# Attention in a hybrid backbone kernel: the transposes of two key tiles issued in one place instead of two

## The chip, the cores and the metric

The kernel runs on one core of one Trainium2 chip. The metric is the device time of one execution in microseconds; the time before the change is the median of three runs. PE is TensorE (PEld its weight loads), DVE is VectorE, ACT is ScalarE, POOL is GpSimd and SP is SyncE, whose queue issues most DMAs.

## The reference, cut to what matters

Two layers over 2048 latent tokens and 256 context tokens. The first is a gated MLP with spatial mixing, the second is windowed attention. Only the attention is touched by the change. For each block of 128 queries, each of 16 heads (4 heads share one set of keys and values) sees the keys of its own block, the block on each side, all 256 context keys and a sink logit:

```python
s_loc = jnp.where(valid, jnp.einsum('bqhgd,bkhd->bhgqk', qb, kb) * scale, NEG_INF)
s_ctx = jnp.einsum('bqhgd,bkhd->bhgqk', qb, k_ctx) * scale
p = jax.nn.softmax(jnp.concatenate([s_loc, s_ctx, s_sink], axis=-1), axis=-1)
out = p_loc @ vb + p_ctx @ v_ctx          # then out * silu(z), the output projection and a layer norm
```

Arithmetic is fp32. The kernel splits an operand into a rounded high part and a low rest, and multiplies the parts on PE.

## The kernel before, in words

Attention is the last stage, from about 2139 us to the end. It goes over 16 query blocks. A block has four **units**, one for each set of keys, and a unit covers four heads. A unit's keys are 5 tiles of 128 (4 in the first and last block), and one key tile of one unit is a **step**: 16 steps in block 0, 20 in each of blocks 1 to 14, 16 in block 15, so 312 in all. Below, the steps of a block of 20 are called 0 to 19; its units begin at steps 0, 5, 10 and 15, and every block begins at an even step of the whole count.

What belongs to a unit and a step:

- `s_mm` (L1087, four matmuls, L1096 to L1099): the scores of one head, into `pS`. `s_max` (L1102, DVE, L1107): adds the mask and finds the extreme. `s_exp` (L1111, ACT, L1115): the exponentials and their sum, in place in the tile `S`; a second, short instruction reads out the sum. Four heads of the next unit are prepared during the steps of the present one.
- `t_mm` (L1118): the four 128x128 transposes (L1122) of a step, one for each head, into one tile `pT` of a PSUM pool that has two buffers (L1030).
- `t_hi` (L1124, ACT, helper line L121): reads `pT` and writes the high part `ph`. `t_lo` (L1129, DVE, helper line L124): `pl` = `pT` minus `ph`. `pl` is the last reader of `pT`, so that a `t_mm` waits for the `pl` of two steps earlier, the last user of its buffer.
- `pv_mm` (L1134, L1139 and L1140): two matmuls of `ph` and `pl` with the values into `pO`, two steps later. After a unit's last tile `o_copy` (L1142, ACT, L1145, tile `ot`) and `o_add` (L1147, DVE, L1151, two additions into `oT`) clear `pO`.
- `out_piece` (L1201, L1216 to L1218): three matmuls of the output projection of the block before into `pY`. The layer norm of that block runs on DVE, ACT (`x`, L575) and POOL (L578, L579). `z_den` (L1157) makes the softmax's denominators on DVE (`es`, L1166) and ACT.

The order on each engine is written out by hand. Every piece of work is entered into a list with a due time in steps, the list is sorted by due time (equal times in the order of entry), and PE, ACT, DVE and POOL each run their instructions in just that order: an instruction that waits holds up all that is behind it on its engine. Within a step s the due times are: `t_mm` at s + 0.25, a score group at s + 0.45, `t_hi` at s + 0.5, the `exp` at s + 0.55, `t_lo` at s + 0.8, `s_max` at s + 0.9, and `pv_mm` of step s at s + 2 (that of a unit's first tile at s + 2.9). At a unit's start at step s the products of the last unit's last tile stand at s + 1, its `o_copy` at s + 1.25 and its `o_add` at s + 1.5.

Of the kernel before, what the change touches and what calls it, by code (L numbers as in the profile page):

```python
# [49 lines left out]
def kernel(  # L50
# [97 lines left out]
    def kk_of(g):  # L148
        return 4 if GROUPS[g][1] == 256 else 2
# [9 lines left out]
    def at(th, g, k):  # L159
        return th[g, k // kk_of(g)][:, k % kk_of(g)]  # L160
# [829 lines left out]
    for g in range(1, NG):  # L990
        s = start_of[0, g - 1]
# [7 lines left out]
    for n in range(1, 5):  # L999
        s, step = start_of[n - 1, 4], 4 * W3  # L1000
        if n == 1:
            s, step = s + 32 * N3, 2 * W3
# [7 lines left out]
    for k in range(7):  # L1010
        s = start_of[4, 2] + 5.4 * k
# [38 lines left out]
    def len_keys(b):  # L1050
        return 4 if b in (0, NB - 1) else 5
# [255 lines left out]
        if ui:  # L1307
            at(first_step[ui - 1] - 3, load_unit, b, kv)
    for s, (b, kv, j) in enumerate(steps):
        at(s + 0.25, t_mm, b, kv, j)  # L1310
        at(s + 0.5, t_hi, b, kv, j)
        at(s + 0.8, t_lo, b, kv, j)
        p = s + 2
        if s >= NS - 2:
            p = NS + (-0.5, 0.6)[s - NS + 2]
        elif s == NS - 3:
            p = NS - 1
        at(p + (0.9 if j == 0 else 0), pv_mm, b, kv, j)
        if j == len_keys(b) - 1:
            fast = b == NB - 1 and kv == 3  # L1320
            at(p + (0.05 if fast else 0.25), o_copy, b, kv)
            at(p + (0.1 if fast else 0.5), o_add, b, kv)
# [37 lines left out]
    b, e = NB - 1, NS  # L1360
# [88 lines left out]
```

## Time and profile before

| | |
|---|---|
| three runs | 2779.89, 2782.4, 2782.86 us (median 2782.4) |
| the profiled execution | 2783.28 us, of it 2781.5 us from the first to the last instruction |
| granted TensorE clock, mean | 0.997 of full speed |
| busy over the span | PE 2734.1 us (98%), DVE 1615.7 (58%), ACT 956.3 (34%), POOL 593.6 (21%) |
| share of the chain of work that ended last | PE 90%, DVE 6%, DMA 2%, ACT 1% |
| from 2500 to 2600 us (inside attention), busy of 100 us | PE 98.09, DVE 87.31, ACT 76.34, POOL 39.78 |

A row of the timeline gives the start, the time it took, the engine, the line, the operation, what is written and read, the shape and the count; in brackets stands the idle time of the engine before it and what ended it. Matmuls are pipelined: four transposes in one row with "0.60" are four starts and the last one's end, and the next row can start before that end. The table shows shares of the whole program; attention's own shares are those of its last line.

### The profile page before, as it was taken

The page shows a single profiled execution, that of the slowest core. Times are in us where ns is not written, and L with a number is a line of the kernel's source. Part 1 is how long each engine was busy: PE and PEld are TensorE (multiplying, and loading weights), DVE is VectorE, ACT ScalarE, POOL GpSimd, SP SyncE. Part 2 cuts the span into 40 slices and gives each one's busy share as a digit, 9 for nine tenths or more (in the row PEclk, how much of TensorE's full clock was granted, in tenths as well). Part 3 has the DMA queues.
Part 4 walks back from the last instruction along what each step waited for, and adds up shares of the span by engine and source line. Part 5 has one row for each costly group of instructions (what it writes and reads, how often), then busy time and mean ns, then how long its engine had stood idle before and what let it go on. Part 6 is the DMA issues. An engine that isn't in the chain of part 4 may idle for free.

```text
span 2781.5 us, 37612 instructions
## 1 busy us (share of the span) xinstructions
PE 2734.1 (98%) x13896; PEld 2321.7 (83%) x13896; DVE 1615.7 (58%) x3225; ACT 956.3 (34%) x1854; POOL 593.6 (21%) x498
## 2 busy tenths in 40 slices
PE   7999999999999999999999999999998999999998
PEld 6788888888888888888888888888887888888886
DVE  7531226556566555465555555455334888888887
ACT  5320222112122112132111113322223777777775
POOL 0000002223222222221111111122100333433343
PEclk9999999999999999999999999999999999999999
DMA  8631332223223323235333336533344444434442
GB/s 318 199 96 50 99 89 92 86 89 106 81 86 106 92 80 98 68 125 180 107 117 114 117 125 225 200 122 110 110 140 137 148 125 132 132 120 125 132 122 69
DMA packets 283069, 338.54 MB, mean 122 GB/s; under 512 B 24579, under 2 KB 190851, under 8 KB 282886
## 3 DMA queue, kind: packets, MB, share of 16 engines
q1 hardware_dynamic: 244006, 316.10, 35.3%
q10 hardware_dynamic: 38880, 20.05, 2.5%
q8 instruction: 109, 1.79, 0.3%
q14 instruction: 74, 0.61, 0.1%
HBM read 232.25 MB, written 103.83 MB: 121 GB/s over the span
## 4 chain that ended last, share of the span: by engine, by line
PE 90%; DVE 6%; DMA 2%; ACT 1%; issue 1%; POOL 0%; SPq 0%; DVEq 0%; ACTq 0%; POOLq 0%
PE pu L376 5%; PE pu L377 5%; PE pv L232 5%; PE pu L378 5%; PE pv L233 5%; PE pv L234 5%; PE pt L740 5%; PE pt L741 5%; PE pt L739 5%; PE pz L376 5%; PE po L618 5%; PE pz L377 5%; PE pz L378 5%; PE po L619 5%; PE po L621 5%; PE pT L1122 4%
## 5 line engine op out<-in xcount | busy, mean ns | idle before, releaser
L124 DVE TENSOR_TENSOR pl<-pT,ph 128x512 fp32r<-128x512 f32 x312 | 214.3, 687 | 79.6 <-ACT ph L121 75.8
L376 PE MATMUL pu<-hh,wuh 128*128 128x512 f32 (+1 forms) x640 | 240.4, 376 | 0.0
L232 PE MATMUL pv<-wvh,hh 128*128 128x512 f32 x576 | 225.2, 391 | 14.6 <-ACT hh L121 14.6
L377 PE MATMUL pu<-hh,wul 128*128 128x512 f32 (+1 forms) x640 | 236.1, 369 | 0.0
L378 PE MATMUL pu<-hl,wuh 128*128 128x512 f32 (+1 forms) x640 | 235.7, 368 | 0.0
L376 PE MATMUL pz<-hh,wzh 128*128 128x512 f32 (+1 forms) x640 | 235.4, 368 | 0.0
L377 PE MATMUL pz<-hh,wzl 128*128 128x512 f32 (+1 forms) x640 | 235.4, 368 | 0.0
L378 PE MATMUL pz<-hl,wzh 128*128 128x512 f32 (+1 forms) x640 | 235.4, 368 | 0.0
L739 PE MATMUL pt<-kh,wbh 128*128 128x512 f32 (+1 forms) x592 | 228.8, 386 | 0.0
L740 PE MATMUL pt<-kh,wbl 128*128 128x512 f32 (+1 forms) x592 | 228.7, 386 | 0.0
L741 PE MATMUL pt<-kl,wbh 128*128 128x512 f32 (+1 forms) x592 | 228.6, 386 | 0.0
L618 PE MATMUL po<-woh,yh 128*128 128x512 f32 x576 | 226.6, 393 | 1.7 <-ACT yh L121 1.7
L619 PE MATMUL po<-wol,yh 128*128 128x512 f32 x576 | 225.1, 391 | 0.0
L233 PE MATMUL pv<-wvl,hh 128*128 128x512 f32 x576 | 224.9, 390 | 0.0
L234 PE MATMUL pv<-wvh,hl 128*128 128x512 f32 x576 | 224.8, 390 | 0.0
L621 PE MATMUL po<-woh,yl 128*128 128x512 f32 x576 | 221.8, 389 | 0.0
L1107 DVE CUSTOM_DVE_ANT_0 S<-pS,mask 128x640 f32<-128x640 f32 (+1 forms) x252 | 216.9, 861 | 3.7 <-PE pS L1099 3.7
L1115 ACT ACTIVATE S<-S,nm 128x640 f32<-128x640 f32 (+1 forms) x240 | 196.7, 820 | 56.4 <-DVE nm L1107 56.2
L467 POOL TENSOR_TENSOR u<-u,z 128x512 f32<-128x512 f32 (+1 forms) x80 | 107.5, 1344 | 490.8 <-DVE z L466 484.7
L121 ACT ACTIVATE ph<-pT 128x512 fp32r<-128x512 f32 x312 | 184.9, 593 | 71.7 <-PE pT L1122 68.3
L1122 PE MATMUL pT<-ident,S 128*128 128x128 f32 x1232 | 186.3, 273 | 9.8 <-DVE pl L124 8.3
L1122 PEld LDWEIGHTS pT<-ident,S 128*128 128x128 f32 x1232 | 151.6, 141 | 46.8 <-DVE pl L124 10.9
(224 smaller groups left out, 5991.2 us busy)
## 6 DMA issues: line engine op xcount, KB each, us to landing
vscr<-vt ACTq DMA_DIRECT2D x72, 256.0 KB, 2.3
yr<-yscr SPq DMA_DIRECT2D x72, 256.0 KB, 3.1
ar<-in_dram SPq DMA_DIRECT2D x64, 256.0 KB, 2.8
vr<-vscr SPq DMA_DIRECT2D x64, 256.0 KB, 2.7
yscr<-y SPq DMA_DIRECT2D x64, 256.0 KB, 2.4
q<-qscr SPq DMA_DIRECT2D x64, 256.0 KB, 3.7
wor<-in_dram SPq DMA_DIRECT2D x46, 256.0 KB, 2.9
kh<-khscr SPq DMA_DIRECT2D x56, 192.0 KB, 3.3
```

Of the source, the lines that this page charges most:

```text
L232: T.matmul(ps, hk[:, cs], wh, start=first, stop=False)
L233: T.matmul(ps, hk[:, cs], wl, start=False, stop=False)
L234: return T.matmul(ps, lk[:, cs], wh, start=False, stop=last)
L376: T.matmul(ps[:, 0:tn], w[0][:, k], at(hh, g, k), start=(k == 0), stop=False)
L377: T.matmul(ps[:, 0:tn], w[1][:, k], at(hh, g, k), start=False, stop=False)
L378: T.matmul(ps[:, 0:tn], w[0][:, k], at(hl, g, k), start=False, stop=(k == KD - 1))
L618: T.matmul(pss[hf], hi[:, c % 4], wh[:, cs], start=(c == 0), stop=False)
L619: T.matmul(pss[hf], hi[:, c % 4], wl[:, cs], start=False, stop=False)
L739: T.matmul(ps, wh[:, cs], at(kh, g, k), start=(k == 0), stop=False)
L740: T.matmul(ps, wl[:, cs], at(kh, g, k), start=False, stop=False)
L741: T.matmul(ps, wh[:, cs], at(kl, g, k), start=False, stop=(k == KD - 1))
L1122: T.transpose(pt[:, hq * P:hq * P + P], u["st"][hq][0][:, j * P:j * P + P], ident)
```

## The change

Step s issued its own transposes at s + 0.25. Now an odd step's transposes are due one step earlier, at the same time as those of the even step ahead of it, and come directly behind them on PE. So eight transposes go out together, into both buffers of `pT`, at every even step, and none at an odd step. All other due times stay.

```diff
     for s, (b, kv, j) in enumerate(steps):
-        at(s + 0.25, t_mm, b, kv, j)
+        at(s - s % 2 + 0.25, t_mm, b, kv, j)
         at(s + 0.5, t_hi, b, kv, j)
         at(s + 0.8, t_lo, b, kv, j)
```

## Rows read from the trace of the kernel before

**Rows 1.** The page's costliest groups: the transposes (busy, mean ns; idle before, releaser).
```profile
L1122 PE MATMUL pT<-ident,S 128*128 128x128 f32 x1232 | 186.3, 273 | 9.8 <-DVE pl L124 8.3
```

**Rows 2.** Windows by stage: stretch, us, busy by engine, PEclk, DMA share, GB/s.
```profile
2139.00:2150.00 11.00, 8.73 (x53) 8.03 (x54) 6.59 (x16) 6.12 (x14) 0.00 (x0) 0.85 0.66 209
...
2180.00:2300.00 120.00, 118.71 (x712) 103.63 (x711) 102.11 (x223) 93.03 (x192) 43.56 (x33) 1.00 0.40 121
...
2700.00:2745.00 45.00, 43.72 (x268) 37.78 (x267) 37.78 (x87) 33.79 (x72) 19.43 (x14) 1.00 0.30 90
```

**Rows 3.** Waits of PE, 2139 to 2782 us: us in total, times, longest.
```profile
PE pT L1122 <- DVE pl L124: 8.3, 13, 0.6
PE pO L1140 <- DVE pl L124: 4.6, 4, 2.8
...
PE pT L1122 <- ACT S L1115: 1.6, 2, 1.1
```

**Rows 4.** Waits of DVE and ACT in the same stretch.
```profile
DVE pl L124 <- ACT ph L121: 75.8, 112, 2.5
ACT ph L121 <- PE pT L1122: 68.3, 124, 3.9
```

**Rows 5.** Timeline of PE, steps 0 to 2 of one block.
```profile
2489.97 0.60 PE L1122 MATMUL pT<-ident,S 128*128 128x128 f32 x4
2490.32 0.42 PE L1096 MATMUL pS<-kh,q 128*128 128x384 f32 x1
2490.58 0.34 PE L1097 MATMUL pS<-kl,q 128*128 128x384 f32 x1
...
2491.23 0.39 PE L1140 MATMUL pO<-pl,vc 128*128 128x512 f32 x1
2491.46 0.60 PE L1122 MATMUL pT<-ident,S 128*128 128x128 f32 x4
...
2493.19 0.60 PE L1122 MATMUL pT<-ident,S 128*128 128x128 f32 x4
```

**Rows 6.** Timeline of ACT, the same steps.
```profile
2491.82 0.19 ACT L1115 ACTIVATION_READ_ACCUMULATOR S<-S,nm 128x1 f32 x1
2492.03 0.60 ACT L1145 ACTIVATE ot<-pO 64x512 f32<-64x512 f32 x1
```

**Rows 7.** Timeline of DVE, the same steps.
```profile
2492.66 0.85 DVE L1151 TENSOR_TENSOR oT<-pO,ot 64x256 f32<-64x256 f32 x2
2493.54 0.69 DVE L124 TENSOR_TENSOR pl<-pT,ph 128x512 fp32r<-128x512 f32 x1
```

**Rows 8.** Timeline of PE, the transposes of steps 4, 6 and 7 of that block.
```profile
2497.44 0.60 PE L1122 MATMUL pT<-ident,S 128*128 128x128 f32 x4
...
2501.93 0.60 PE L1122 MATMUL pT<-ident,S 128*128 128x128 f32 x4
...
2503.76 0.66 PE L1122 MATMUL pT<-ident,S 128*128 128x128 f32 x4 [0.64 <-DVE pl L124]
```

**Rows 9.** Timeline of ACT, steps 4 and 5.
```profile
2498.24 0.19 ACT L1115 ACTIVATION_READ_ACCUMULATOR S<-S,nm 128x1 f32 x1
2498.33 0.58 ACT L121 ACTIVATE ph<-pT 128x512 fp32r<-128x512 f32 x1
...
2498.91 1.24 ACT L575 ACTIVATE x<-x,bnb,brs 128x1024 f32<-128x1024 f32 x1
```

**Rows 10.** Timeline of POOL, the layer norm of an earlier block.
```profile
2500.22 2.40 POOL L578 TENSOR_TENSOR x<-x,st 128x1024 f32<-128x1024 f32 x1 [2.27 <-ACT x L575]
```

**Rows 11.** Timeline of DVE, steps 3 to 5.
```profile
2497.97 0.68 DVE L124 TENSOR_TENSOR pl<-pT,ph 128x512 fp32r<-128x512 f32 x1
...
2499.55 0.88 DVE L1107 CUSTOM_DVE_ANT_0 S<-pS,mask 128x640 f32<-128x640 f32 x1
...
2500.35 2.30 DVE L1166 TENSOR_TENSOR es<-es,l 128x8 f32<-128x8 f32 x1
...
2503.05 0.65 DVE L124 TENSOR_TENSOR pl<-pT,ph 128x512 fp32r<-128x512 f32 x1
```

## The prediction

> **What bounds the kernel now.** I read the windows by stage first. From 2180 to 2745 us, the steady part of attention, PE is busy 97 to 99% of each stretch at a granted clock of 1.00, DVE about 85%, ACT 75 to 78% [rows 2]. So PE sets the end, and what the change can win is what PE still waits. The waits of PE come next: 8.3 us of transposes waiting for DVE's `pl`, in 13 places of 0.64 us, one in nearly every block; 4.6 us of products in 4 places and 1.6 us on the exponentials in 2 [rows 3]. Against that stand idle times that cost nothing today: DVE 75.8 us until `ph`, ACT 68.3 us until the transposes [rows 4]. Last I read the timelines of PE, ACT and DVE through one block, because with two `pT` buffers the question is when each `pl` lands.
>
> **The change, part by part.**
>
> *The transposes themselves.* No instruction is added or removed, no DMA moves, and SP and POOL are passed by nothing. A group of four holds PE for 0.44 us: the next row starts 0.35 us after it (2489.97 to 2490.32) and then needs 0.42 where its like needs 0.34 [rows 5]. If the extra 0.08 were a switch from transposes to other matmuls, joining 156 pairs would save 156 x 0.08 = 12.5 us. But four transposes take 0.60 us and one takes 273 ns [rows 1, 5], so that they start (600 - 273) / 3 = 109 ns apart, and 0.44 / 4 is 110 ns: the 0.08 is the fourth transpose's own time. I take nothing, and keep 12.5 us of gain for the range.
>
> *The new wait.* The odd step's group needs the buffer of the odd step before, so it waits for that step's `pl`. Until now it had a whole step's work of PE in front of it. Now it has one group, 0.44 us. Behind it in PE's queue wait scores (and so `s_max` and the exponentials), a projection piece and products.
>
> At steps 2 and 3 I lay the same rows out in the new order. The pair at step 0 starts at 2489.97 as before. The products of the last unit's last tile ended at 2491.23 + 0.39 = 2491.62 [rows 5] and now end one group later, at 2492.06. ACT is free at 2491.82 + 0.19 = 2492.01 and started `ot` at 2492.03 [rows 6]; now it starts at about 2492.09, 0.03 us behind the products, as `oT` starts 0.03 us behind `ot` (2492.63 to 2492.66). `oT` follows 0.63 us after `ot`'s start and `pl` of step 1 0.88 us after that [rows 6, 7], so that `pl` runs from 2493.60 to 2494.29. From `pl`'s end to the transposes that waited for it is 0.06 us (2503.70 to 2503.76) [rows 8, 11], so step 3's group can start at 2494.35. PE has done the same work up to step 2, in another order, and starts that group at 2493.19 [rows 5]; it is ready for step 3's at 2493.63. **PE waits 0.72 us.** That happens where a unit begins at an even step, that is at steps 3 and 13, twice in each of 14 blocks: 28 x 0.72 = 20.2 us.
>
> *Step 5* is the first tile of a unit, and its transposes, one step earlier, need the fourth head's exponentials. These end at 2498.24 + 0.19 = 2498.43 [rows 9], and the group would have come at 2497.44 + 0.44 = 2497.88 [rows 8], a wait of 0.6 us. But PE is by then 0.72 us later and the DVE and ACT work that leads there only 0.06, so nothing is left.
>
> *Steps 6 and 7.* Here PE waits 0.64 us already, since `pl` of step 5 is late: ACT's layer norm ends at 2500.15, POOL's L578 starts at 2500.22, and DVE's tiny `es` addition, begun 0.13 us later, lasts until L578 is done, 2.30 us [rows 9 to 11]. In the new order step 4's transposes start 0.72 us later, at 2498.16, and `ph` 0.63 us after that (0.60 and the same 0.03), 0.46 us after its old start [rows 8, 9]. The layer norm, L578, `es` and `pl` of step 5 move with it, and `pl` ends at 2503.70 + 0.46 = 2504.16; step 7's group can start at 2504.22. PE reaches it at 2501.93 + 0.72 + 0.44 = 2503.09 [rows 8], since the scores that stood between steps 6 and 7 (0.67 - 0.08 = 0.59 us) now come behind. It waits 1.13 us. Group and scores end at 2504.22 + 0.44 + 0.59 = 2505.25 instead of 2504.20, so that PE is now 1.05 us late and not 0.72: 0.33 us more in 13 blocks, 4.3 us. The bounds are 0 and 0.75 (with the old times of `pl`, 1.39 less 0.64), or 0 to 9.8 us.
>
> *The other pairs.* `pl` of the odd step comes earlier than now, since its transposes do, and PE comes later; I take 0. *Blocks 0 and 15* have eight units that begin at even steps: up to 8 x 0.72 = 5.8 us, while the 4.6 + 1.6 = 6.2 us of waits that don't repeat by block [rows 3] could go. I take 0 between these.
>
> **Sum.** 20.2 + 4.3 = 24.5 us on the profiled execution's own 2783.28 us, which gives 2807.8; that execution is 0.9 us over the median of the runs shown, so the forecast is 2807 us.
>
> **The rivals.**
>
> *The `es` addition gets in front of L578.* It begins 0.13 us behind it [rows 10, 11], and both move. `s_max`, which holds `es` up, starts when `pl` of step 4 is off DVE. If DVE comes out 0.13 us or more ahead, `pl` of step 5 is some 2 us earlier and step 7's wait is gone: PE's lag there falls from 1.05 to -0.08 us, 13 x 1.13 = 14.7 us less, or 2792. For it speaks how narrow the margin is; against it, that both hang on step 4's `ph` and move together.
>
> *No catching up.* If each `pl` stays where it is, every pair pays what today's times show: at step 2, 2494.23 + 0.06 - 2493.63 = 0.66; at step 4, 2498.65 + 0.06 - 2497.88 = 0.83; at step 6 a net 0.75; at step 12 about as much as at step 2 [rows 5, 7, 8, 11]. That is 2.9 us a block, 41 us or 2823, and more with the pairs not shown. It holds where ACT and DVE are short of time, not just kept waiting; rows 4 speak against it.
>
> *The lead pays off (not slower).* The odd steps' transposes are ready early, ACT and DVE use up idle time [rows 4] and no `pl` is late any more. Then the 8.3 and 1.6 us of waits of rows 3 go: 2772. Its point is DVE's queue ahead of `pl` of step 1: that `pl` must end by 2493.57, 0.72 us sooner than laid out. Against it: `pl` follows `oT` by 0.03 us, with no idle time before it [rows 7], and `oT` depends on products that the change puts later.
>
> *The clock falls.* Today it reads 1.00 with 13 waits of 0.64 us, and 0.85 only at the stage's start, among waits of up to 2.8 us [rows 2, 3]; there it cost 0.15 x 11 = 1.65 us. One such loss a block would add 23 us, 2830. The longest wait that I lay out is 1.13 us, so I give it little. The Trainium skill (TensorE: Matmul & The Clock Gate, "A second HAM failure mode: psum-queue depth-cycling") tells of a kernel in which brief idle times between groups of matmuls that cycled through PSUM banks made the clock swing between its levels. By that rule the time would be this rival's; the trace before, which has such waits at full clock, does not agree so far.
>
> That the change does something else than it says I leave out: equal due times keep the order of entry.
>
> **How the numbers follow.** Forecast 0.64, `es` in front 0.14, no catching up 0.10, the lead pays off 0.08, clock 0.04. The forecast's own range is 2797 (step 7 costs nothing, half of the 12.5 us is real) to 2818 (9.8 us at step 7, 5.8 in the outer blocks). To hold 8 in 10 I reach to the `es` case below, 2790, and to the no-catching-up case above, 2826. A measurement can tell about 0.2%, 5.6 us, from no change. Faster has 0.05, from the lead; the same 0.07, 0.03 from the lead and 0.04 from the `es` case's lower edge; slower 0.88.
>
> **What would show it.** Right: waits of the transposes on `pl` rise from 8.3 us to 35 or more (20.2 + 13 x 1.13 = 34.9, and some in the outer blocks), as 0.72 us at steps 3 and 13 and 1.1 at step 7, the second group alone waiting; ACT's waits on transposes fall; the clock stays at 1.00; a block takes some 1.8 us more. Wrong: `es` at 0.17 us in most blocks (the first rival), waits at steps 5, 9 or 15 (no catching up), or PE's waits below 10 us.

## The result, and the profile after

The changed kernel takes 2813.83 us (median of 4 runs, 2809.97 to 2815.72) against 2782.18 us (4 runs, 2779.89 to 2782.86) for the kernel before: a ratio of 1.0114, 95% interval 1.01 to 1.0129. It is slower by about 32 us, where 2807 us had been forecast. The profiled execution took 2812.83 us, 29.55 us more than the one of before; its mean granted clock is again 0.997.

All of the loss is in attention. From one block's first transposes to the next's, the block of [rows 5] took 39.6 us and now takes 41.6. Blocks 1 to 14 together went from 554.4 to 580.7 us, 26.3 us more; the rest of the 29.55 us lies in blocks 0 and 15.

PE's waits from 2139 us to the end (us in total, times, longest), to be held against [rows 3]:

```profile
PE pT L1122 <- DVE pl L124: 44.4, 48, 3.5
PE pS L1097 <- DMA kl<-klscr: 0.9, 1, 0.9
PE pS L1096 <- DVE pl L124: 0.8, 1, 0.8
```

13 waits of 8.3 us have become 48 of 44.4 us. In blocks 1 to 14 they stand in three places only: step 3 (14 times), step 13 (14 times) and step 7 (13 times). The other seven are in blocks 0 and 15. The 4.6 us of products waiting for `pl` are gone from the table. It lists idle time of PE, so a group that starts late while the last transposes are still under way is not in it; step 5 below is such a place.

The windows by stage show the other side (us, busy by engine, clock, DMA share, GB/s), to be held against [rows 2]: every engine is less busy in a stretch, and the clock has not moved.

```profile
2180.00:2300.00 120.00, 114.52 (x679) 100.04 (x678) 96.44 (x209) 87.61 (x183) 40.67 (x30) 1.00 0.40 118
...
2700.00:2745.00 45.00, 42.59 (x254) 37.16 (x253) 36.15 (x78) 32.56 (x69) 15.56 (x11) 1.00 0.39 121
```

**Steps 0 to 3**, in the same block as [rows 5 to 7]. PE, with the eight transposes of steps 0 and 1, the second of the last unit's two products, and the transposes of steps 2 and 3:

```profile
2505.89 1.03 PE L1122 MATMUL pT<-ident,S 128*128 128x128 f32 x8
...
2507.58 0.40 PE L1140 MATMUL pO<-pl,vc 128*128 128x512 f32 x1
...
2509.10 0.60 PE L1122 MATMUL pT<-ident,S 128*128 128x128 f32 x4
2510.36 0.63 PE L1122 MATMUL pT<-ident,S 128*128 128x128 f32 x4 [0.66 <-DVE pl L124]
```

ACT, then DVE, over the same steps:

```profile
2508.02 0.60 ACT L1145 ACTIVATE ot<-pO 64x512 f32<-64x512 f32 x1
```

```profile
2508.65 0.85 DVE L1151 TENSOR_TENSOR oT<-pO,ot 64x256 f32<-64x256 f32 x2
2509.52 0.69 DVE L124 TENSOR_TENSOR pl<-pT,ph 128x512 fp32r<-128x512 f32 x1
```

Read from the first transposes, at 2505.89: the products end at 2507.98, `ot` starts 0.04 us after that, `oT` 0.63 us after `ot`, `pl` of step 1 0.87 us after `oT`, and `pl` ends at 2510.21, which is 4.32 us in. The second group of the next pair would have been ready at 2509.10 + 0.44 = 2509.54 and starts at 2510.36. The stall is 0.82 us. The row's bracket says 0.66, because it counts from the end of the last transpose (2509.70), which comes 0.16 us after PE could have begun the next.

**Steps 4 to 7**, to be held against [rows 8 to 11]. PE:

```profile
2514.17 1.24 PE L1122 MATMUL pT<-ident,S 128*128 128x128 f32 x8
...
2518.75 0.60 PE L1122 MATMUL pT<-ident,S 128*128 128x128 f32 x4
2520.40 0.63 PE L1122 MATMUL pT<-ident,S 128*128 128x128 f32 x4 [1.06 <-DVE pl L124]
```

POOL, then DVE:

```profile
2516.77 2.40 POOL L578 TENSOR_TENSOR x<-x,st 128x1024 f32<-128x1024 f32 x1 [2.83 <-ACT x L575]
```

```profile
2513.96 0.68 DVE L124 TENSOR_TENSOR pl<-pT,ph 128x512 fp32r<-128x512 f32 x1
...
2516.91 2.29 DVE L1166 TENSOR_TENSOR es<-es,l 128x8 f32<-128x8 f32 x1
...
2519.61 0.65 DVE L124 TENSOR_TENSOR pl<-pT,ph 128x512 fp32r<-128x512 f32 x1
```

The pair of steps 4 and 5 takes 1.24 us where that of steps 0 and 1 takes 1.03: step 5's group starts 0.15 us behind `pl` of step 3, which ends at 2514.64, and so 0.18 us late. It is 0.18 to 0.21 us late in blocks 2 to 14, 2.5 us in all, and the table of waits has none of it.

L578 still gets in ahead of `es`, by 0.14 us where it was 0.13, and `es` ends when L578 does, 0.03 us after it, in each of these 13 blocks. The Trainium skill (GPSIMD Engine Reference, "8. Key points") says that GpSimd shares its SBUF interfaces with VectorE, with contention for VectorE instructions that have two SBUF inputs; `es` is one, and the rows agree (2.29 us beside L578, 0.17 us where no POOL instruction runs). The price that the rows show is the whole remainder of the POOL instruction: in block 15, where `es` starts 1.45 us behind L578, it takes 0.95 us, again until L578 ends.

### The profile page after: what moved, and what is told of

Its sections match the earlier page's. It is cut to its first block, busy times and chain, and to the rows that moved or that the text cites. A ratio compares the mean times of both kernels' runs of the same rounds, so it can differ in the third digit from the quotient of the medians.

```text
span 2811.0 us, 37681 instructions
## 1 busy us (share of the span) xinstructions
PE 2736.0 (97%) x13896; PEld 2325.8 (83%) x13896; DVE 1614.6 (57%) x3225; ACT 953.4 (34%) x1854; POOL 592.0 (21%) x498
## 4 chain that ended last, share of the span: by engine, by line
PE 90%; DVE 6%; ACT 1%; DMA 1%; issue 1%; POOL 0%; SPq 0%; DVEq 0%; ACTq 0%; POOLq 0%
PE pu L376 5%; PE pu L377 5%; PE pv L232 5%; PE pu L378 5%; PE pv L234 5%; PE pv L233 5%; PE pt L741 5%; PE pt L739 5%; PE pt L740 5%; PE pz L376 5%; PE po L618 5%; PE pz L377 5%; PE pz L378 5%; PE po L619 5%; PE po L621 5%; PE pT L1122 4%
## 5 line engine op out<-in xcount | busy, mean ns | idle before, releaser
L124 DVE TENSOR_TENSOR pl<-pT,ph 128x512 fp32r<-128x512 f32 x312 | 213.7, 685 | 107.9 <-ACT ph L121 106.1
L1122 PE MATMUL pT<-ident,S 128*128 128x128 f32 x1232 | 172.2, 274 | 44.1 <-DVE pl L124 43.7
L121 ACT ACTIVATE ph<-pT 128x512 fp32r<-128x512 f32 x312 | 184.2, 591 | 66.3 <-PE pT L1122 64.5
L1122 PEld LDWEIGHTS pT<-ident,S 128*128 128x128 f32 x1232 | 142.0, 141 | 74.5 <-PE pT L1122 31.9
```

The source lines that it names most:

```text
L1122: T.transpose(pt[:, hq * P:hq * P + P], u["st"][hq][0][:, j * P:j * P + P], ident)
```

## The experiments

The kernel before was run again beside each experiment; its median was 2781.54 us for the first four and 2782.08 us for the second four. Edits are shown against the changed kernel, unless the kernel before is named.

### Which pairs cost: leave out four of a block's ten

```diff
-        at(s - s % 2 + 0.25, t_mm, b, kv, j)
+        own = s % 2 and j in (0, 3)
+        at(s - (0 if own else s % 2) + 0.25, t_mm, b, kv, j)
```

> Steps 3 and 13 of a block (the fourth tile of a unit that begins at an even step) and steps 5 and 15 (the first tile of a unit that begins at an odd step) get their own place back; six of a block's ten pairs stay. Theory (the wait sits only where pl of the unit's second tile is queued behind oT, steps 3 and 13, and behind the es addition, step 7): PE's waits at steps 3 and 13 go, 2 x 0.83 us in 14 blocks = 23 us; step 7 waits 1.39 us with its scores now behind it, 0.59 us more than before the change, 13 x 0.59 = 8 us; so 2790 us, within 4. Rival 1 (every pair costs, because ACT and DVE have no time left): the six pairs that stay take over the waits, 2805 us or more, with waits at steps 9, 11, 17 or 19. Rival 2 (eight transposes in a row cost by themselves): 6/10 of the 31 us stay, 2801 us.

Measured: 2792.65 us, ratio to before 1.0039 (1.0024 to 1.0054). PE's waits:

```profile
PE pT L1122 <- DVE pl L124: 16.5, 14, 1.2
PE pO L1140 <- DVE pl L124: 4.1, 5, 2.4
```

21 of the 32 us are back. Products wait for `pl` again, as in the kernel before (second row). Of the 14 waits of transposes that remain 13 are at step 7 and one in block 0. Six pairs a block still go out together, five of them without any wait, so neither pairing as such nor eight transposes in a row is what costs. Step 7's wait has grown as the theory said: its scores no longer stand in front of it.

```profile
2308.86 0.66 PE L1122 MATMUL pT<-ident,S 128*128 128x128 f32 x4 [1.23 <-DVE pl L124]
```

### What makes `pl` late at steps 3 and 13: `ot` and `oT` moved behind it

For units that end at an odd step, `ot` and `oT` come behind `ph` and `pl` of the next unit's second tile (and one multiplication on POOL that reads `oT` moves by 0.06 of a step, to stay behind it).

```diff
-            at(p + (0.05 if fast else 0.25), o_copy, b, kv)
-            at(p + (0.1 if fast else 0.5), o_add, b, kv)
+            late = p % 2 == 1 and not fast
+            at(p + (0.05 if fast else 0.52 if late else 0.25), o_copy, b, kv)
+            at(p + (0.1 if fast else 0.85 if late else 0.5), o_add, b, kv)
...
-            at(z + (-3, -0.1)[hf], y_mul, b, *ks)
+            at(z + (-3, -0.04)[hf], y_mul, b, *ks)
```

> All pairs stay; for units that end at an odd step, ot moves behind ph and oT behind pl of the next unit's second tile. Theory (the chain PV products, ot, oT, pl makes the wait at steps 3 and 13): those waits fall from 0.66 us to under 0.15 as the profile shows them, 23 us of stall go; in their place the first tiles at steps 5 and 15 can wait for the exponentials, at most 0.6 us each (17 us), and step 7 stays; 2790 to 2806 us. Rival 1 (pl is late for want of DVE time, not because of that chain): the waits at steps 3 and 13 stay above 0.5 us and the time is 2810 us or more.

Measured: 2790.6 us, 1.0033 (1.002 to 1.0046). DVE at steps 1 and 2, and PE there: `pl` of step 1 now follows `s_max` directly, with `oT` behind it, and the eight transposes of steps 2 and 3 go out in one run.

```profile
2498.44 0.69 DVE L124 TENSOR_TENSOR pl<-pT,ph 128x512 fp32r<-128x512 f32 x1
2499.05 0.84 DVE L1151 TENSOR_TENSOR oT<-pO,ot 64x256 f32<-64x256 f32 x2
```

```profile
2498.98 1.04 PE L1122 MATMUL pT<-ident,S 128*128 128x128 f32 x8
...
2504.57 0.63 PE L1122 MATMUL pT<-ident,S 128*128 128x128 f32 x4 [0.76 <-DVE pl L124]
```

The waits at steps 3 and 13 are gone: the chain is the cause of them. The time falls by 23 us, but these two places are not all of it. In the profiled execution 28 x 0.82 = 23.0 us go there and 13 x 0.55 = 7.2 us go at step 7, whose wait shrinks from 1.06 to 0.51 us (it was expected to stay), while others come up at step 5; blocks 1 to 14 fall by 17.7 us in all. The second row shows the wait at step 5, a stall of 0.76 + 0.16 = 0.92 us. It stands there as the theory allowed, but it is for `pl` of step 3 and not for the exponentials. In the changed kernel the same `pl` cost 0.18 us there; the 0.82 us at step 3 are likely to have covered the rest.

### What makes `pl` late at step 7: the `es` addition moved past the layer norm

```diff
-            for i, t in enumerate((0.15, 1.1, 2.1)):
+            for i, t in enumerate((0.15, 1.1, 4.3 if hf == 0 and 0 < b < NB - 1 else 2.1)):
```

> The changed kernel, with the first half's es addition, reciprocal and transpose of blocks 1 to 14 two steps later (behind pl of step 7), past the two POOL multiplications and additions of the layer norm. Theory: es takes 0.17 us instead of 2.29, the wait at step 7 goes (1.06 us as the profile shows it, 1.21 of stall, in 13 blocks: 16 us), those at steps 3 and 13 stay: 2798 us, within 4. Rival 1 (DVE is short of time in any case): waits move to steps 5 and 9 and the time falls by less than half of that, 2806 or more.

Measured: 2800.69 us, 1.0066 (1.0051 to 1.0081). `es` over the steady stretch (count; busy us, mean ns), then PE's waits:

```profile
L1166 DVE TENSOR_TENSOR es<-es,l 128x8 f32<-128x8 f32 x29 | 5.6, 193 | 0.0
```

```profile
PE pT L1122 <- DVE pl L124: 30.2, 38, 2.3
```

The mean of `es` falls from 1148 to 193 ns and no wait is left at step 7. Those at steps 3 and 13 stand as they were. Blocks 1 to 14 fall from 580.7 to 566.3 us, 14.4 of the 16 expected, since step 15's group now starts up to 0.4 us late in six of the blocks, 1.6 us together. Blocks 0 and 15 were some 4 us slower in this profiled execution than in that of the changed kernel. There the granted clock read 0.50 in three stretches where the changed kernel's did not; two of them follow waits of 1.93 us (block 0) and 1.89 us (block 15) for `pl` (windows as in [rows 2]):

```profile
2172.90:2176.20 3.30, 3.30 (x13) 2.91 (x11) 2.47 (x6) 2.63 (x5) 1.28 (x1) 0.50 0.39 115
2760.00:2763.40 3.40, 3.40 (x12) 2.72 (x11) 0.78 (x3) 0.72 (x3) 0.10 (x1) 0.50 0.53 180
```

### The same edit to the kernel before

> The kernel before with the same later es addition. Theory: the 13 waits of 0.64 us (0.80 of stall with the drain) at step 7 go and nothing takes their place: 10 us, 2772. Rival: PE, at 98%, or another wait takes it back: 2779 or more.

Measured: 2768.96 us (5 runs), 0.9957 (0.9943 to 0.9971). PE's waits now hold no transposes waiting for `pl`:

```profile
PE pO L1140 <- DVE pl L124: 3.7, 4, 2.2
PE pT L1122 <- ACT S L1115: 2.2, 3, 1.1
PE pS L1096 <- DMA q<-qscr: 2.0, 1, 2.0
PE pY L1218 <- DVE yl L124: 1.1, 1, 1.1
```

This is the lowest median of the study, faster than both kernels. In the profiled executions blocks 1 to 14, where the addition was moved, fall from 554.4 to 543.6 us: 10.8 us, near the 10 expected. Most of the rest lies ahead of them, where nothing was moved: the profile of the kernel before has four short stretches at granted clock 0.50 there, this one has none.

### Pairs of the other parity

```diff
-        at(s - s % 2 + 0.25, t_mm, b, kv, j)
+        at(s - ((s + 1) % 2 if 0 < b < NB - 1 and s > 16 else 0) + 0.25, t_mm, b, kv, j)
```

> In blocks 1 to 14 an even step's transposes come directly behind those of the odd step ahead of it (blocks 0 and 15 as in the kernel before). Theory (the wait sits at the second pair after a unit's start, where pl is queued behind oT): the units that begin at odd steps now pay, with waits at steps 8 and 18 of 0.66 us or more as the profile shows them (at step 8 more, since the long es addition stands ahead of the same pl), and none at steps 3 and 13, where the unit begins inside a pair; 2805 to 2820 us. Rival (it is the even steps, or the place in the block, that matters): waits stay in the neighbourhood of steps 3 and 13 or spread over all pairs.

Measured: 2833.45 us, 1.0187 (1.017 to 1.0204). The places are as expected: 14 waits at step 8 and 14 at step 18, none at steps 3 and 13 (and 13 short ones each, 0.2 us, at steps 4 and 7, and three more in blocks 1 and 2). The time is 13 us over the upper end. Here are step 7 and step 8 in one block, and then three windows of that block (us; busy of PE, PEld, DVE, ACT, POOL; clock; DMA share; GB/s):

```profile
2315.33 0.66 PE L1122 MATMUL pT<-ident,S 128*128 128x128 f32 x4 [0.19 <-DVE pl L124]
2317.70 1.09 PE L1122 MATMUL pT<-ident,S 128*128 128x128 f32 x4 [1.71 <-DVE pl L124]
```

```profile
2310.00:2317.50 7.50, 5.79 (x35) 4.83 (x33) 7.09 (x14) 5.71 (x12) 4.76 (x2) 1.00 0.31 90
2317.60:2320.90 3.30, 3.20 (x11) 2.94 (x12) 1.35 (x3) 1.40 (x3) 0.00 (x0) 0.50 0.67 214
2321.00:2328.00 7.00, 6.96 (x42) 5.96 (x42) 4.49 (x10) 4.09 (x9) 1.94 (x2) 1.00 0.40 131
```

Behind the wait of 1.71 us the granted clock is 0.50, its lower level of 1.2 GHz, where it is otherwise 1.00, 2.4 GHz. The wait at step 8 is 0.66 us in block 1 and 1.71 us in the 13 others, and in 8 of these 13 the clock falls behind it. A 3.3 us stretch at half clock loses some 1.65 us of work, and the blocks show it: blocks 4 to 7 and 11 to 13, with such a stretch, take 44.0 to 44.1 us, blocks 3 and 8 to 10, without, 42.5. The eight together are 8 x 1.65 = 13 us, as much as the time lies over the upper end of the expectation, which had left the clock out.

### The second group half a step later

```diff
-        at(s - s % 2 + 0.25, t_mm, b, kv, j)
+        at(s - 0.5 * (s % 2) + 0.25, t_mm, b, kv, j)
```

> Pairs as in the changed kernel, but the odd step's transposes stand half a step later, behind the even step's scores, which are 0.59 us of PE's work. Theory (what costs is how soon the second group comes after the first): the stall of 0.83 us at steps 3 and 13 falls to about 0.2, step 7 is back to the kernel before's 0.64 us row, and the time is 2785 us, within 4. Rival (the run-ahead itself crowds ACT and DVE): above 2795. A side question is the handover from pl's end to the waiting transposes, 0.06 us in the kernel before, where scores went ahead of the group, and 0.15 us in the changed kernel, where transposes did: if what went ahead decides it, it is 0.06 here.

Measured: 2783.36 us (10 runs), 1.0008 (0.9998 to 1.0017). One group of scores between the two groups is enough to take the loss away. No wait is left at steps 3 and 13, where 0.2 us had been expected; 13 of the 30 stand at step 7 (0.48 us) and 11 at step 5 (0.16 us). PE's waits, then step 7 on DVE and PE:

```profile
PE pT L1122 <- DVE pl L124: 15.9, 30, 1.9
```

```profile
2305.79 0.65 DVE L124 TENSOR_TENSOR pl<-pT,ph 128x512 fp32r<-128x512 f32 x1
```

```profile
2306.49 0.66 PE L1122 MATMUL pT<-ident,S 128*128 128x128 f32 x4 [0.48 <-DVE pl L124]
```

The side question, the time from `pl`'s end to the waiting transposes, gives 2306.49 - 2306.44 = 0.05 us here, the short value. What goes ahead on PE is still not the answer: in the first experiment step 7's group also followed transposes directly, and its `pl`, 2308.15 to 2308.80, was followed 0.06 us later by the 2308.86 shown above. What goes with the long handover is a further instruction. In the changed kernel, by the transposes' line, PE's sequencer runs these, and the kernel before has none:

```profile
L1122 PEldq EVENT_SEMAPHORE  x127: 51/51/51, 2144.1 to 2789.1; - x127
```

At the stalled groups of the changed kernel such an instruction waits for DVE, and the weight load behind it waits for a second semaphore. At step 7 of the first experiment there is none. The two go together without exception: over the traces of both kernels and all experiments, the 185 groups that waited for `pl` behind such an instruction started 0.14 to 0.15 us after it, the 66 without one 0.05 to 0.06 us. That the 0.09 us between the two handovers come from this was not tried by itself.

### Both mends together

The edits of the second and third experiments, on the changed kernel.

> The changed kernel with both mends: ot and oT behind the second tile's ph and pl, and the es addition two steps later. Theory (the two queues found are the whole cost): what is left is the wait at step 5 that came up with the first mend (0.76 us as the profile shows it, some 0.9 of stall, in 13 blocks: 12 us) over the 2769 us of the kernel before with the later es addition, so 2781 us, or 2770 if that wait goes too. Rival (pairing has another cost): 2790 or more.

Measured: 2783.24 us (10 runs), 1.0008 (0.9998 to 1.0017). The waits that are left are those of step 5, 13 of them at 0.76 us, and eight others.

```profile
PE pT L1122 <- DVE pl L124: 16.5, 21, 1.0
```

The time is 2 us over the 2781 us expected and does not reach the rival's 2790. So the two queues carried the loss of the change as it was made. Pairs are not free with both mends, though: the same kernel without pairs and with the later `es` takes 2769 us, and the 14 us between them are mostly the wait at step 5 (13 x 0.92 = 12.0 us).

### The pairs that wait for nothing

The first experiment's edit with the later `es`.

> The six pairs of a block that stayed in the first experiment, with the later es addition. Theory (a pair whose pl is in time costs nothing and gains nothing, since a group of transposes takes 0.44 us wherever it stands): the 2769 us of the kernel before with the later es addition, within 3. Rival (joining two groups saves a switch of 0.08 us): 6/10 of 156 pairs x 0.08 = 7 us less, 2762.

Measured: 2771.53 us (5 runs), 0.9968 (0.9955 to 0.9981), within the scatter of the 2768.96 us without pairs (0.9943 to 0.9971). Two rows of PE show pairs that went out in one run:

```profile
2299.85 1.04 PE L1122 MATMUL pT<-ident,S 128*128 128x128 f32 x8
...
2303.53 1.04 PE L1122 MATMUL pT<-ident,S 128*128 128x128 f32 x8
```

Eight transposes start within 1.04 - 0.27 = 0.77 us, 7 x 110 ns. No transposes wait for `pl` in this trace, and blocks 2 to 13 take 38.77 to 38.81 us each, against 38.73 to 38.90 without pairs. A pair in time costs nothing and gains nothing; the 7 us of a saved switch do not appear.

## Why the prediction was right, step by step

**The transposes themselves: nothing.** Right, shown by the last experiment. The 12.5 us kept in the range for a saved switch are not there.

**Steps 3 and 13: 0.72 us each, 20.2 us.** Right in place, cause and number of times: 28 waits, in the two places named, and they go when `ot` and `oT` are moved. `pl` of step 1 was laid out to end 4.32 us after the pair's start and ended there. The size is 0.82 us, 28 x 0.82 = 23.0 us. The term that was mis-sized is the handover from `pl` to the transposes, taken as 0.06 us from a group that waited for one semaphore and measured at 2510.36 - 2510.21 = 0.15. That no instruction is added did not hold either: the 127 sequencer instructions shown above are new, and they go with the longer handover.

**Step 5: no wait.** Right of the exponentials, and nearly right of the time: the group starts 0.18 to 0.21 us late in 13 blocks, 2.5 us. The prediction looked at the exponentials alone; the group waits for `pl` of step 3, its buffer's last reader. With the stall at step 3 out of the way, in the second experiment, that wait grew to 0.92 us.

**Step 7: 1.13 us instead of 0.80, 4.3 us in all.** Measured: the group was ready at 2518.75 + 0.44 = 2519.19 and began at 2520.40, a stall of 1.21 us, 13 x 0.41 = 5.3 us more than before. The difference is the same handover.

**The other pairs of a block: nothing.** Right: no wait in blocks 1 to 14 stands anywhere else, and no other second group there starts more than 0.06 us late.

**Blocks 0 and 15: nothing.** Wrong, and the second term mis-sized, though the range had up to 5.8 us for them. Between their first transposes and the next block's, block 0 went from 32.7 to 34.1 us; from the first transposes to those of its fifteenth step block 15 went from 29.4 to 31.9. That is 3.8 us, of which 0.7 come back behind it. There every unit begins at an even step, and seven waits stand at their fourth tiles. The first experiment, which splits those pairs too, has them back at 32.7 and 29.4.

**The sum.** 24.5 us were forecast on the profiled execution and 29.55 came. The handover adds 2.8 + 1.0 = 3.8 us, step 5 adds 2.5 and the outer blocks 3.1. Some 4.5 us come off in blocks 1 to 14: the stalls there add up to 23.0 + 5.3 + 2.5 = 30.8 us, and 26.3 were measured. Of these 4.5, 1.1 us are the wait on the exponentials at the start of block 1, which is gone; where the others lie stays open. So the errors cancel in part, but the forecast does not live by that: without the 4.5 us the sum would still lie in the range.

**The rivals.** `es` did not get in front of L578; the 0.13 us of margin held, because both hang on step 4's `ph`, which was the argument against. No catching up: waits at three places and not at all pairs, so it falls, and the split settles it. The lead does not pay off: ACT's waits for the transposes fall only from 68.3 to 64.5 us, DVE's for `ph` rise from 75.8 to 106.1. The clock stayed at 1.00 in blocks 1 to 14, with waits up to 1.06 us, and also behind the waits of 1.92 us (block 0) and 1.90 us (block 15), as these windows show:

```profile
2170.00:2176.00 6.00, 4.82 (x31) 4.35 (x32) 5.12 (x12) 4.52 (x11) 1.29 (x1) 1.00 0.31 81
...
2770.30:2775.00 4.70, 4.67 (x28) 3.91 (x28) 2.71 (x7) 2.60 (x6) 2.47 (x2) 1.00 0.38 133
```

The one stretch at 0.50 inside block 0, at 2156 us, is in the kernel before as well. So the clock has no part in the loss of the profiled execution. But the third and fifth experiments show that this rival was real and near, for behind waits of 1.7 to 1.9 us the clock fell in some places and not in others. The rule of the Trainium skill that stood beside it (TensorE: Matmul & The Clock Gate, "A second HAM failure mode: psum-queue depth-cycling") tells of brief idle times of PE in a cycle through PSUM banks with a clock that swings. The fifth experiment agrees with it in part: idle times at the `pT` buffers and a clock that falls and rises again, but once a block of 42 to 44 us. In the changed kernel itself the trace did not agree with it, and by it the 23 us of that rival would have come on top.

## What to carry to other kernels

Before moving an instruction forward on the engine that sets the end, ask which of its buffers' last readers is still queued, on which engine, and behind what; with two buffers, filling both at once leaves PE no work to cover the reader with, and here one group of other work between the two fills (the scores, 0.59 us) was enough. A forward move cost nothing where the reader was in time, so the places to lay out are those where another chain stands ahead of it. The rows of one block gave nearly all of it here; the first and last block, which are built otherwise, cost 3.1 us that those rows did not show. When one such wait is taken away, look for the next: behind step 3 stood step 5. The gain here lay elsewhere: a tiny addition on DVE that was caught behind a POOL instruction cost 11 to 13 us, while no arrangement of the transposes won anything.

## What was not expected of the hardware

A DVE addition of 128x8 elements, 0.17 us by itself, takes 2.3 us when it starts 0.13 us behind a POOL instruction of 2.4 us, in 13 blocks out of 14: it ends when the POOL instruction does. Moving it took 13 us off 2782, of which 10.8 lie in the blocks where it was moved. A group that waits for one semaphore starts 0.05 to 0.06 us after `pl` ends; one that has a second to wait for, with a further sequencer instruction of 51 ns, starts after 0.14 to 0.15. All 251 such waits in these traces fall into one or the other. And a PE wait of 1.71 us, once a block in otherwise dense work, was in 8 blocks of 13 followed by a stretch at half clock, while the waits of 1.06 us (the changed kernel) and 1.23 us (the first experiment) at step 7 never were. The length of the wait alone doesn't decide: in the other 5 blocks the clock stayed up, and a wait of 1.9 us in block 15 was followed by half clock in the third experiment and not in the changed kernel.
